# A hybrid block with a mixture of experts: another order of work on TensorE, fp32r slot tables, other PSUM banks for second blocks

## The chip, the cores and the metric

One core of a Trainium2 chip runs the whole program. The metric is the device time of one execution in microseconds (us), smaller is better. The kernel before takes 2412.09 us in the median of 3 runs (2403.3 to 2412.42).

A core has five engines with a queue of instructions each, which they work through in order: TensorE (PE, matrix products and transposes), VectorE (DVE), ScalarE (ACT), GpSimd (POOL) and SyncE (SP). An instruction that waits holds up everything behind it on its engine. SP issues most DMA transfers, POOL and ACT a few; a transfer waits until its buffer is free, and what stands behind it in that queue waits too.

## The reference

One layer over 2048 tokens of width 1024, with 256 context tokens, in float32. Cut to what matters:

```python
m  = silu(c) @ w_mod + b_mod            # six rows: sh1, sc1, g1, sh2, sc2, g2; the context has its own
hn = modulate(rmsnorm(h, g_norm1), sh1, sc1)
cn = modulate(rmsnorm(cx, g_norm1), csh1, csc1)
z  = hn @ w_in                          # u, v (512 each), q (256), r (512), k (256), v (512), gates (32)
# context: k, v, gates only; its two final states start the scans over the latent tokens
a_out = spatial_gating(z_u, z_v, ...)   # gelu, group norm, a 128x128 product per group and chunk
o     = gla_bidir(q, k, v, la_f, la_b, s_ctx_f, s_ctx_b)   # chunks of 64, states carried both ways
b_out = rmsnorm(o) * g_gla * silu(z_r)
h     = h + g1 * (concat([a_out, b_out]) @ w_out)
hn2   = modulate(rmsnorm(h, g_norm2), sh2, sc2)
# hierarchical MoE: best of 8 groups, the best 2 of its 8 experts, blocks of 128 tokens per expert
y = segment_sum(gate * (silu(x @ w1[e]) * (x @ w3[e])) @ w2[e])
out = rmsnorm(h + g2 * y, g_final)
```

## The kernel before

**Precision.** A float32 product is built from values split into a high and a low part of type fp32r: `mm3` (lines 84 to 86) issues high x high, high x low and low x high. ACT makes the high part (`split_w`, L80), DVE the low part by a subtraction (L81). Where rows are few, plain float32 products are used, for example for the ranks and slot tables of the routing.

**Tiles and stages.** The 2048 tokens are 16 tiles of 128 rows, numbered 0 to 15 (T is 15); the 2 tiles of the context are -2 and -1, and two tiles make a pair, -1 for the context and 0 to 7 for the rest. The order of the work is written out by hand, function by function, and each engine's queue follows it.

- *Prologue and stage A* (to about 505 us). `kv_mm` makes k, v and gate columns of one tile in 8 steps over the width, six products each; `zg_t` transposes the gate columns (`pz`), `lg_mm` makes the decay logits (`lg`, then ACT and DVE make `la`), `pb_mm` sums them (`pr_`, `pb`, `pd`), and `pkv_mm` makes the state update (`pkv`, then `sf` on DVE). `xtr(0, g)` transposes pair 0 into the operands `xh` and `xl`. `ua_split(i)` splits two raw tiles of the u and v weights (`raw`, four buffers, loaded at L443). Then a loop over pairs; the last `psx_mm`, `q_mm` and `r_mm` calls stand at L586 to L594.
- *Stage C* (505 to 766 us), tile 15 down to 0: `c_q`, `c_qt`, `c_att` (scores `paf`, `pab`, masked into `at`), `c_o` (`po`), `c_r`, `c_bt` (transposes `pbt`, copied to `mfc` and sent to memory as `mxD`). In between run the splits of the output weights, and the modulation vectors (`mod2`: a row `macc` is set to zero, gets a bias row by DMA at L725, and is summed up by two DVE instructions a step at L728).
- *Stage D* (to about 1031 us), again from tile 15 down: `d_load` fetches a tile of `mxD`, `d_split` makes its parts `mhd` and `mld`, `d_mm`/`d_mix` multiply by the output weights, `d_norm` normalises, `d_logit` and `d_route` choose experts, `d_rank` counts a token's place in its expert (`prk`, against a running count `coh`), and `d_tab` adds to the table `slots`, which holds for every slot of every expert the token and the gate: `at` (one-hot of the place) times `what` (one-hot of the expert, scaled by the token or by the gate). The last two tiles go side by side (`lanes`, L1139). The finished table gives `idx` and `gate`, and POOL gathers the first experts' rows with `idx` (L1163).
- *MoE*, 64 experts in turn. `xprep` transposes the gathered rows (128x128 each) into one pair of PSUM banks and splits them; `block` multiplies; `yevac` (L1218) empties the output banks `PY` with the gate. Seven experts have more than 128 tokens and so a second block: its `xprep` goes through `PY`, and its up-products accumulate in the banks `TP`, which the first blocks' `xprep` uses.

## Time and profile before

| | |
|---|---|
| median of 3 runs | 2412.09 us |
| profiled execution | 2410.06 us, span 2408.4 us |
| PE busy | 2259.7 us (94%) |
| DVE busy | 1932.1 us (80%) |
| ACT busy | 1437.3 us (60%) |
| POOL busy | 739.2 us (31%) |

The profile is of one execution. Its own time is 1.7 us above its span, and 2.0 us under the median of the runs. PE is busy for nearly all of the span, so what matters is where it is idle, and where its clock is granted at half: a busy PE at half clock takes twice as long for the same products.

### The profile page before, as it was taken

Reading aid. Unit: us, or ns where it says so; the run is one execution under the profiler, and the core shown is the slowest. Engines: PE = TensorE matmul, PEld = TensorE weight load, DVE = VectorE, ACT = ScalarE, POOL = GpSimd, SP = SyncE. Lnnn points to the kernel's source line nnn. Section 1 sums busy time; section 2 is a strip of 40 time slices with the busy share of each in tenths; the row PEclk is TensorE's granted clock in tenths of the full one; section 3 lists DMA queues with packets and bytes.
Section 4 is the critical chain, followed back from the end, with each engine's and each line's share of the span. In section 5 each row is a group of like instructions: output and inputs, shape, how many; then the busy total and the mean of one; then the engine's idle time right before and its main releaser. Section 6 shows DMA issues by size and latency. Waiting matters only on the chain.

```text
span 2408.4 us, 40084 instructions
## 1 busy us (share of the span) xinstructions
PE 2259.7 (94%) x11932; PEld 1860.0 (77%) x11932; DVE 1932.1 (80%) x4302; ACT 1437.3 (60%) x2731; POOL 739.2 (31%) x602
## 2 busy tenths in 40 slices
PE   8999999989999899899999999999999999999990
PEld 3888888977777788778777888888777788888870
DVE  4556665657786888789887899999686699999986
ACT  3544444432332222378676788888575688888873
POOL 1123311146673122237431222323131132322220
PEclk9899999989999999989999999999999999999995
DMA  7333322356675654589997899999996799999947
GB/s 274 105 107 106 121 92 97 109 170 210 219 241 175 227 210 159 184 323 374 323 310 259 292 377 372 365 352 348 325 327 194 223 360 373 368 358 363 360 140 296
DMA packets 193220, 613.42 MB, mean 255 GB/s; under 512 B 36557, under 2 KB 36685, under 8 KB 192854
## 3 DMA queue, kind: packets, MB, share of 16 engines
q1 hardware_dynamic: 152358, 516.56, 59.0%
q0 software_dynamic: 38048, 87.95, 12.4%
q10 hardware_dynamic: 2448, 4.46, 0.5%
q8 instruction: 178, 2.92, 0.5%
q14 instruction: 188, 1.54, 0.2%
HBM read 547.42 MB, written 102.28 MB: 270 GB/s over the span
## 4 chain that ended last, share of the span: by engine, by line
PE 35%; DVE 11%; DMA 6%; issue 5%; ACT 1%; DVEq 0%; another core or an unknown queue 0%; SPq 0%; POOLq 0%; ACTq 0%; POOL 0%
DVE wl L81 9%; PE pa L84 7%; PE pa L86 7%; PE pa L85 7%; DMA we<-in_w_e_dram 3%; PE py L84 2%; PE py L85 2%; PE py L86 2%; DMA accD<-y,idx 2%; PE tpe L1196 1%; PE tpe L85 1%; PE tpe L84 1%; PE tpe L86 1%; DVE y L1218 1%; ACT wh L80 1%
## 5 line engine op out<-in xcount | busy, mean ns | idle before, releaser
L81 DVE TENSOR_TENSOR wl<-we,wh 128x512 fp32r<-128x512 f32 x1536 | 967.6, 732 | 82.5 <-ACT wh L80 76.2
L80 ACT ACTIVATE wh<-we 128x512 fp32r<-128x512 f32 x1536 | 892.9, 630 | 146.3 <-DVE wl L81 46.3
L84 PE MATMUL pa<-wh,xhe 128*128 128x512 f32 x1024 | 404.2, 395 | 9.5 <-ACT wh L80 7.5
L1221 POOL DMA_INDIRECT accD<-y,idx x71 | 245.7, 3460 | 525.0 <-DVE y L1218 440.5
L86 PE MATMUL pa<-wh,xle 128*128 128x512 f32 x1024 | 400.4, 391 | 0.0
L85 PE MATMUL pa<-wl,xhe 128*128 128x512 f32 x1024 | 399.9, 391 | 0.0
L84 PEld LDWEIGHTS pa<-wh,xhe 128*128 128x128 f32 x1024 | 192.6, 188 | 69.9 <-issue 28.6
L86 PEld LDWEIGHTS pa<-wh,xle 128*128 128x128 f32 x1024 | 192.6, 188 | 41.0
L1163 POOL DMA_INDIRECT xg<-hnD,idx x64 | 96.5, 1508 | 410.7 <-DVE wl L81 124.9
L85 PEld LDWEIGHTS pa<-wl,xhe 128*128 128x128 f32 x1024 | 192.8, 188 | 37.6
L84 PE MATMUL py<-wh,hhe 128*128 128x512 f32 x512 | 213.5, 417 | 6.7 <-ACT wh L80 6.2
L86 PE MATMUL py<-wh,hle 128*128 128x512 f32 x512 | 202.7, 396 | 1.5 <-issue 1.3
L85 PE MATMUL py<-wl,hhe 128*128 128x512 f32 x512 | 201.1, 393 | 2.9 <-DVE wl L81 2.9
L86 PEld LDWEIGHTS py<-wh,hle 128*128 128x128 f32 x512 | 97.0, 190 | 25.3 <-issue 3.1
L351 POOL TENSOR_SCALAR sc<-sc,dec 64x128 f32<-64x128 f32 x140 | 111.1, 793 | 17.8 <-PE po L683 6.4
L84 PEld LDWEIGHTS py<-wh,hhe 128*128 128x128 f32 x512 | 97.4, 190 | 24.5 <-issue 6.1
L85 PEld LDWEIGHTS py<-wl,hhe 128*128 128x128 f32 x512 | 97.7, 191 | 16.0
L1071 POOL DMA_INDIRECT tabD<-pair,ri x32 | 70.0, 2189 | 91.4 <-DMA tabD<-pair,ri 59.0
L1218 DVE SCALAR_TENSOR_TENSOR y<-py,gate,g2b 128x512 f32<-128x512 f32 x128 | 93.0, 791 | 4.0 <-PE py L86 3.9
L86 PE MATMUL pmx<-hi,mld 128*128 128x512 f32 x224 | 89.0, 397 | 6.1 <-DVE mld L81 6.1
L84 PE MATMUL pmx<-hi,mhd 128*128 128x512 f32 x224 | 91.9, 410 | 1.7 <-ACT mhd L80 1.7
L85 PE MATMUL pmx<-lo,mhd 128*128 128x512 f32 x224 | 88.0, 393 | 0.0
(417 smaller groups left out, 4651.2 us busy)
## 6 DMA issues: line engine op xcount, KB each, us to landing
we<-in_w_e_dram SPq DMA_DIRECT2D x765, 512.0 KB, 9.9
wt<-in_w_modB_dram SPq DMA_DIRECT2D x32, 512.0 KB, 5.7
kve<-kveD SPq DMA_DIRECT2D x48, 256.0 KB, 5.5
wt<-in_w_modA_dram SPq DMA_DIRECT2D x16, 512.0 KB, 7.5
x<-in_x_dram SPq DMA_DIRECT2D x16, 512.0 KB, 3.8
xD<-xf POOLq DMA_DIRECT2D x32, 256.0 KB, 3.1
mfd<-mxD SPq DMA_DIRECT2D x16, 512.0 KB
xd<-in_x_dram SPq DMA_DIRECT2D x16, 512.0 KB, 5.0
```

The lines of the kernel that those rows point to most:

```text
L80: act.activation(hi, raw, AF.Copy)
L81: vec.tensor_tensor(lo, raw, hi.bitcast(F32), op=OP.subtract)
L84: pe.matmul(o, lh, wh, start=start, stop=False)
L85: pe.matmul(o, lh, wl, start=False, stop=False)
L86: pe.matmul(o, ll, wh, start=False, stop=stop)
L351: pool.tensor_scalar(s1[64:128, hs], s0[64:128, hs], dec[64:128, ci, h:h + 1], None, op0=OP.mult)
L1071: pool.indirect_dma_start(out=tabD, out_offset=bass.IndirectOffsetOnAxis(ap=ri[:, i:i + 1], axis=0), in_=pair[:, i], in_offset=None)
L1163: pool.indirect_dma_start(out=x, out_offset=None, in_=hnD, in_offset=bass.IndirectOffsetOnAxis(ap=ix, axis=0), bounds_check=S - 1, oob_is_ ...
L1196: pe.transpose(four(tp[c // 4])[:, c % 4], x[:, c * P:(c + 1) * P], ident)
L1218: vec.scalar_tensor_tensor(y[:, c], py[i], gt, g2b[:, c], op0=OP.mult, op1=OP.mult)
L1221: pool.indirect_dma_start(out=accD, out_offset=bass.IndirectOffsetOnAxis(ap=ix, axis=0), in_=y, in_offset=None, bounds_check=S - 1, oob_is ...
```

## The change

Six edits.

1. *Prologue.* `xtr(0, 0)`, `xtr(0, 1)`, `pkv_mm(t0)`, `kv_mm(0, 0)` and `pkv_mm(-1)` stand at other places among the context's steps.
2. *End of stage A.* `q_mm(14)` stands ahead of `psx_mm(7, 0)`, `psx_mm(7, 1)` stands in the middle of `r_mm(15)`; the first half of `r_mm(14)` is cut into two pieces, the second behind `c_att(15)`.
3. *End of stage C.* The products `d_mm(15, 0)` stand ahead of `c_o(0)` and `d_mm(15, 1)` ahead of `c_bt(0)`; the splits of tiles 15 and 14 are made a step earlier, and tile 13's `mfd` is loaded with them into a buffer of another pool.
4. *Slot tables.* `ot`, `coh`, `at`, `what` and two constant matrices become fp32r, so the products of `d_rank` and `d_tab` are fp32r. The gate is split into a high and a low column, so `what` has 192 columns where it had 128: more ACT instructions, one on DVE, and at the end one more to add the two parts.
5. *Last routing chain.* `warm` multiplies constants into banks that nothing reads: 5 products ahead of the last ranks, 1 ahead of the last tables, 3 behind the counts.
6. *Second blocks.* Their `xprep` goes through `TP` where it went through `PY`.

```diff
--- before.py
+++ after.py
@@ -469,23 +469,25 @@
     kv_mm(-1, 1, 0, 4)
     lg_mm(t0)
     ua_split(1)
-    xtr(0, 0)
     kv_mm(-1, 1, 4, KD)
     ptt = pt("aux", [P, 4, P], "ptt")
     for g in range(4):
         pe.matmul(ptt[:, g], lnb[:, g * P:(g + 1) * P], wsp[:, g], start=True, stop=False)
         pe.matmul(ptt[:, g], ones[0:1], bsp[:, g * P:(g + 1) * P], start=False, stop=True)
     vec.tensor_copy(tt, ptt)
-    xtr(0, 1)
+    xtr(0, 0)
     zg_t(t1)
     pb_mm(t0)
+    xtr(0, 1)
     ua_split(2)
     xtr(0, 2)
-    lg_mm(t1)
-    ua_split(3)
     pkv_mm(t0)
     xtr(0, 3)
     xload(1)
+    ua_split(3)
+    kv_mm(0, 0, 0, 4)
+    lg_mm(t1)
+    kv_mm(0, 0, 4, KD)
     pb_mm(t1)
     for i in range(4, 8):
         ua_split(i)
@@ -493,12 +495,12 @@
     for pr in range(NP):
         t0, t1 = 2 * pr, 2 * pr + 1
         nx = pr + 1 < NP
-        kv_mm(pr, 0, 0, KD)
         if pr:
+            kv_mm(pr, 0, 0, KD)
             psx_mm(pr - 1, 0)
-        else:
+        kv_mm(pr, 1, 0, 2)
+        if not pr:
             pkv_mm(-1)
-        kv_mm(pr, 1, 0, 2)
         zg_t(t0)
         kv_mm(pr, 1, 2, 4)
         if pr:
@@ -584,14 +586,15 @@
             mm3(RP[ti], *lhs(ti // 2, ti % 2, k), rh[k], rl[k], k == 0, k == KD - 1)
 
     q_mm(T)
+    q_mm(T - 1)
     psx_mm(NP - 1, 0)
-    q_mm(T - 1)
     c_kv(T)
     c_s0(T, 1)
     back(2 * (T + NCT) + 1, "kb")
     c_s0(T, 0)
+    r_mm(T, 0, 4)
     psx_mm(NP - 1, 1)
-    r_mm(T, 0, KD)
+    r_mm(T, 4, KD)
     es.close()
 
 
@@ -760,7 +763,12 @@
         oh_.append(hi)
         ol_.append(lo)
 
-    MX, MF, XR, PM = {}, [], {}, {}
+    MX, MF, MFD, XR, PM = {}, [], {}, {}, {}
+
+    def warm(o, n):
+
+        for _ in range(n):
+            pe.matmul(o, ident, cst[:, 0:512], start=True, stop=True)
 
     def d_x(ti, pl=None, tag="xd"):
         x = XR[ti] = (pl or wk).tile([P, D], F32, name="xd", tag=tag, **({} if pl else {"bufs": 2}))
@@ -780,12 +788,13 @@
     msk = cload("msk", [P, 2, P], dt=I32, p=wk)
     mod2_load(0)
     c_q(T)
-    r_mm(T - 1, 0, 4)
+    r_mm(T - 1, 0, 2)
     c_r(T)
     c_qt(T)
     c_kv(T - 1)
     c_st(T - 1)
     c_att(T)
+    r_mm(T - 1, 2, 4)
     for it in range(NT):
         ti = T - it
         n = ti - 1
@@ -795,6 +804,8 @@
             if it:
                 q_mm(n)
             c_q(n)
+        if n < 0:
+            d_mm(T, 0)
         c_o(ti)
         if n >= 0:
             if it:
@@ -812,7 +823,14 @@
             c_kv(n - 1)
             c_st(n - 1)
         if n < 0:
-            d_mm(T, 0)
+            d_mm(T, 1)
+        if it == NT - 2:
+            for i in range(2):
+                MX[T - i] = [wa.tile([P, KD, P], F32R, name=f"mx{j}", tag="w") for j in range(2)]
+                split_w(MF[i], *MX[T - i])
+                d_x(T - i, wa, "w")
+            MFD[T - 2] = wa.tile([P, KD, P], F32, name="mfd", tag="w")
+            sp.dma_start(out=MFD[T - 2], in_=mxD[T - 2])
         c_bt(ti)
         if n >= 0:
             c_att(n)
@@ -831,31 +849,27 @@
                 mf = wk.tile([P, KD, P], F32, name="mfd", tag="x", bufs=2)
                 sp.dma_start(out=mf, in_=mxD[T - i])
                 MF.append(mf)
-        if it == NT - 2:
-            for i in range(2):
-                MX[T - i] = [wa.tile([P, KD, P], F32R, name=f"mx{j}", tag="w") for j in range(2)]
-                split_w(MF[i], *MX[T - i])
-                d_x(T - i, wa, "w")
-    d_mm(T, 1)
     for j in range(2):
         d_mm(T - 1, j)
     es.close()
     p1s.close()
 
 
-    coh = const.tile([P, NE], F32, name="coh")
-    vec.memset(coh, 0.0)
+    coh = const.tile([P, NE], F32R, name="coh")
+    cohf = coh.bitcast(F32)
+    vec.tensor_scalar(coh, cst[:, 0:NE], 0.0, None, op0=OP.mult)
     zero = const.tile([P, 1], F32, name="zero")
     vec.memset(zero, 0.0)
     es = ExitStack()
     wk = es.enter_context(tc.tile_pool(name="p1d", bufs=1))
+    lor = wk.tile([P, 2, P], F32R, name="lor")
+    vec.tensor_copy(lor.rearrange("p t c -> p (t c)"), cst[:, 5 * P:7 * P])
+    lowr, onesr = lor[:, 0], lor[:, 1]
     bc = [wk.tile([P, D], F32, name=f"bc{i}") for i in range(2)]
     wr = wk.tile([P, KD, G + NE], F32, name="wr")
     br = wk.tile([P, G + NE], F32, name="br")
     iota = wk.tile([P, NE], F32, name="iota")
     HH, HN, HT = ({} for _ in range(3))
-
-    MFD = {}
 
     def d_load(ti):
         mf = MFD[ti] = wk.tile([P, KD, P], F32, name="mfd", tag="x", bufs=2)
@@ -1001,7 +1015,7 @@
         vec.tensor_tensor(oh, iota[:, None, :].to_broadcast([P, 2, NE]), ef[:, :, None].to_broadcast([P, 2, NE]),
                           op=OP.is_equal)
         yield
-        ot = wk.tile([P, NE], F32, name="ot", tag="ot", bufs=2)
+        ot = wk.tile([P, NE], F32R, name="ot", tag="ot", bufs=2)
         vec.tensor_tensor(ot, oh[:, 0], oh[:, 1], op=OP.add)
         yield
         RT[ti] = e2, se, ot, oh, ef
@@ -1010,13 +1024,13 @@
         e2, se, ot, oh, ef = RT[ti]
         dn = sm("dn")
         prk = pt("aux", [P, NE], "prk")
-        pe.matmul(prk, low, ot, start=True, stop=False)
+        pe.matmul(prk, lowr, ot, start=True, stop=False)
         for m in more_:
-            pe.matmul(prk, ones, m, start=False, stop=False)
-        pe.matmul(prk, ones, coh, start=False, stop=True)
+            pe.matmul(prk, onesr, m, start=False, stop=False)
+        pe.matmul(prk, onesr, coh, start=False, stop=True)
         pair = const.tile([P, 2, 2], F32, name="pair", tag="pair", bufs=3)
         pool.tensor_copy(pair[:, :, 0], tok[:, ti:ti + 1].to_broadcast([P, 2]))
-        what = wk.tile([P, 2, 2, NE], F32, name="what", tag="what", bufs=2)
+        what = wk.tile([P, 2, 3, NE], F32R, name="what", tag="what", bufs=2)
         act.activation(what[:, :, 0], oh, AF.Copy, scale=tok1[:, ti:ti + 1])
         vec.scalar_tensor_tensor(dn, e2, 1.0, se, op0=OP.add, op1=OP.mult)
         yield
@@ -1024,14 +1038,19 @@
         yield
         vec.tensor_tensor(pair[:, 1, 1:2], pair[:, 0, 1:2], e2, op=OP.mult)
         yield
+        gh, gl = wk.tile([P, 2], F32R, name="gh", tag="gh", bufs=2), sm("gl", 2)
+        act.activation(gh, pair[:, :, 1], AF.Copy)
+        vec.tensor_tensor(gl, pair[:, :, 1], gh.bitcast(F32), op=OP.subtract)
+        yield
         for i in range(2):
-            act.activation(what[:, i, 1], oh[:, i], AF.Copy, scale=pair[:, i, 1:2])
-        rk, at = sm("rk", 2), wk.tile([P, 2, 2 * P], F32, name="at", tag="at", bufs=2)
+            act.activation(what[:, i, 1], oh[:, i], AF.Copy, scale=gh[:, i:i + 1].bitcast(F32))
+            act.activation(what[:, i, 2], oh[:, i], AF.Copy, scale=gl[:, i:i + 1])
+        rk, at = sm("rk", 2), wk.tile([P, 2, 2 * P], F32R, name="at", tag="at", bufs=2)
         ri = const.tile([P, 2], I32, name="ri", tag="ri", bufs=3)
         prod = wk.tile([P, 2, NE], F32, name="prod", tag="prod", bufs=2)
         vec.tensor_tensor(prod, oh, prk[:, None, :].to_broadcast([P, 2, NE]), op=OP.mult)
         yield
-        vec.tensor_tensor(coh, coh, ot, op=OP.add)
+        vec.tensor_tensor(coh, cohf, ot.bitcast(F32), op=OP.add)
         yield
         vec.tensor_reduce(rk, prod, axis=AX.X, op=OP.add)
         yield
@@ -1078,7 +1097,7 @@
         if it > 1:
             d_x(ti)
         if it == 2:
-            slots = pt("mm", [P, 2, 2, NE], "slots")
+            slots = pt("mm", [P, 2, 3, NE], "slots")
             vec.memset(slots, 0.0)
         if it == 1:
             d_split(ti - 1)
@@ -1113,7 +1132,6 @@
             d_tr(ti + 1)
         ss = d_norm(ti, route)
         if it == 0:
-            d_load(T - 2)
             d_load(T - 3)
             pool.dma_start(out=hnD[0:P], in_=sh2b)
             sp.dma_start(out=sh2T, in_=bcD[1:2].rearrange("o (k p) -> p (o k)", p=P))
@@ -1136,8 +1154,11 @@
     rs0 = d_norm0(ss)
     for x in xgr + xqr:
         act.activation(x, zero.to_broadcast([P, D]), AF.Copy)
+    wm = pt("tp", [P, 512], "wm")
+    warm(wm, 5)
     lanes(g_route(1), g_route(0, rs0))
     lanes(g_rank(1), g_rank(0, RT[1][2]))
+    warm(wm, 1)
     d_tab(1)
     d_tab(0)
     wload(NW)
@@ -1147,7 +1168,9 @@
     none = wk.tile([P, 2, NE], F32, name="none")
     vec.tensor_scalar(none, slots[:, :, 0], 0.0, off, op0=OP.is_equal, op1=OP.mult)
     vec.scalar_tensor_tensor(idx.rearrange("p (b e) -> p b e", b=2), slots[:, :, 0], -1.0, none, op0=OP.add, op1=OP.add)
-    vec.tensor_copy(gate.rearrange("p (b e) -> p b e", b=2), slots[:, :, 1])
+    ghi = wk.tile([P, 2, NE], F32, name="ghi")
+    vec.tensor_copy(ghi, slots[:, :, 1])
+    vec.tensor_tensor(gate.rearrange("p (b e) -> p b e", b=2), ghi, slots[:, :, 2], op=OP.add)
     es.close()
 
 
@@ -1174,8 +1197,9 @@
     PA, TP, PY, TH = ([psp.tile([P, 512], F32, name=f"{n}{i}") for i in range(2)] for n in ("pa", "tpe", "py", "th"))
     four = lambda t: t.rearrange("p (c n) -> p c n", c=4)
     pc = TH[1][:, 0:NE]
-    pe.matmul(pc, ones, coh, start=True, stop=True)
+    pe.matmul(pc, ones, cohf, start=True, stop=True)
     ci_ = wk.tile([1, NE], I32, name="ci_")
+    warm(PA[1], 3)
     vec.tensor_scalar(ci_, pc[0:1], float(P - 1), None, op0=OP.add)
     vec.tensor_scalar(nblk, ci_, 7, None, op0=OP.logical_shift_right)
     most = wk.tile([1, 1], I32, name="most")
@@ -1317,7 +1341,7 @@
         base = hpos[e, 0, 0]
 
         def two():
-            xprep(xq[e % 2], rows2(e), PY)
+            xprep(xq[e % 2], rows2(e), TP)
             block(base, 2 * KD, (PA, TP), (xhl, rows2(e)), at)
             glu(PA, sh)
             glu(TP, sh2[e % 2])
```

**Where instructions stand, PE in the prologue.** Before, from the last of the bias products (`ptt`) to the first products of tile 0: `tp` are the transposes of `xtr`, `pz` of `zg_t`; `pr__` and `pd` belong to `pb_mm`.

```order
L477 MATMUL ptt<-bsp,cst 128x128
L213 MATMUL tp<-cst,x 128x128 x4
L254 MATMUL pz<-cst,kz 96x128
L278 MATMUL pr__599<-lah,trs 128x256
L278 MATMUL pr__599<-lal,trs 128x256
L278 MATMUL pr__599<-lah,trs 128x256
L278 MATMUL pr__599<-lal,trs 128x256
L287 MATMUL pd<-chm,la 128x2 x4
L213 MATMUL tp<-cst,x 128x128 x4
L259 MATMUL lg<-wup,zgT_178 128x512
L322 MATMUL pkv<-vv,kd 128x128 x8
L213 MATMUL tp<-cst,x 128x128 x4
```

After, from the same place:

```order
L476 MATMUL ptt<-bsp,cst 128x128
L213 MATMUL tp<-cst,x 128x128 x4
L254 MATMUL pz<-cst,kz 96x128
L278 MATMUL pr__586<-lah,trs 128x256
L278 MATMUL pr__586<-lal,trs 128x256
L278 MATMUL pr__586<-lah,trs 128x256
L278 MATMUL pr__586<-lal,trs 128x256
L287 MATMUL pd<-chm,la 128x2 x4
L213 MATMUL tp<-cst,x 128x128 x8
L322 MATMUL pkv<-vv,kd 128x128 x8
L213 MATMUL tp<-cst,x 128x128 x4
L84 MATMUL kg<-hi,xh 128x288
```

The first four transposes of pair 0 stood between the two halves of `kv_mm(-1, 1)` before, and now all sixteen stand behind it; `lg` has moved behind the first half of `kv_mm(0, 0)`, which begins at the last row.

**SP at the start of stage D.** Before, from the last loads of stage C: `mfd` are tiles of `mxD`, `wt` weights of the modulation, `macc` the bias row.

```order
L832 DMA mfd<-mxD 128x1024 x2
L767 DMA xd<-in_x_dram 128x1024 x2
L872 DMA bc_8286<-bcD 128x1024
L872 DMA bc_8287<-bcD 128x1024
L880 DMA wr<-in_w_r_dram 128x576
L883 DMA iota<-in_iota_dram 128x64
L884 DMA br<-in_b_r_dram 128x72
L713 DMA wt_8311<-in_w_modB_dram 128x1024
L713 DMA wt_8313<-in_w_modB_dram 128x1024
L862 DMA mfd<-mxD 128x1024 x2
L1119 DMA sh2T<-bcD 128x8x1
L725 DMA macc<-in_b_mod_dram 1x1024
```

After:

```order
L775 DMA xd<-in_x_dram 128x1024 x2
L833 DMA mfd<-mxD 128x1024
L886 DMA bc_8290<-bcD 128x1024
L886 DMA bc_8291<-bcD 128x1024
L894 DMA wr<-in_w_r_dram 128x576
L897 DMA iota<-in_iota_dram 128x64
L898 DMA br<-in_b_r_dram 128x72
L716 DMA wt_8315<-in_w_modB_dram 128x1024
L716 DMA wt_8317<-in_w_modB_dram 128x1024
L876 DMA mfd<-mxD 128x1024
L1137 DMA sh2T<-bcD 128x8x1
L728 DMA macc<-in_b_mod_dram 1x1024
```

One of the two `mfd` loads ahead of `sh2T` has moved up, ahead of the `bc` loads; the rest keep their order.

**PE at the end of the routing.** Before, from the last logits (`pl`) to the first expert's transposes (`tpe`):

```order
L945 MATMUL pl<-wr,ht 128x72 x8
L1013 MATMUL prk<-ot,cst 128x64
L1016 MATMUL prk<-coh,cst 128x64
L1013 MATMUL prk<-ot,cst 128x64
L1015 MATMUL prk<-ot,cst 128x64
L1016 MATMUL prk<-coh,cst 128x64
L1064 MATMUL slots<-what,at 128x128 x8
L1177 MATMUL th_11189<-coh,cst 128x64
L1279 TENSOR_LOAD nblk x2
L1196 MATMUL tpe_11184<-cst,xg_10935 128x128 x4
```

After:

```order
L959 MATMUL pl<-wr,ht 128x72 x8
L771 MATMUL wm<-cst 128x512 x5
L1027 MATMUL prk<-ot,lor 128x64
L1030 MATMUL prk<-coh,lor 128x64
L1027 MATMUL prk<-ot,lor 128x64
L1029 MATMUL prk<-ot,lor 128x64
L1030 MATMUL prk<-coh,lor 128x64
L771 MATMUL wm<-cst 128x512
L1083 MATMUL slots<-what,at 128x192 x8
L1200 MATMUL th_11296<-coh,cst 128x64
L771 MATMUL pa_11290<-cst 128x512 x3
```

Three groups of constant products are new, and the tables' products have 192 columns.

## Rows read from the trace of the kernel before

**Rows 1.** Timeline of PE in the prologue: start, duration, what, idle time and releaser.

```profile
58.99 1.47 PE L213 MATMUL tp<-cst,x 128*128 128x128 f32 x4 [2.61 <-DVE x L195]
...
77.61 2.07 PE L322 MATMUL pkv<-vv,kd 64*128 64x128 f32 x14 [3.18 <-DVE la L265]
```

**Rows 2.** Busy time by stretch: stretch, length, engines, granted clock, DMA share, GB/s.

```profile
58.24:65.07 6.83, 5.96 (x20) 5.11 (x21) 4.88 (x8) 2.67 (x6) 0.80 (x1) 0.50 0.26 82
75.30:88.95 13.65, 10.75 (x46) 9.57 (x47) 9.71 (x22) 8.68 (x17) 2.24 (x4) 0.50 0.56 179
```

**Rows 3.** Timeline of DVE in the prologue: the last weight splits.

```profile
91.46 1.36 DVE L81 TENSOR_TENSOR lo<-raw,hi 128x512 fp32r<-128x512 f32 x2 [0.24 <-ACT hi L80]
```

**Rows 4.** Timeline of PE where stage A ends.

```profile
506.56 2.05 PE L395 MATMUL psx<-wsp,ga 128*128 128x128 f32 x8 [3.73 <-DVE sf L335]
...
522.23 0.60 PE L659 MATMUL pqt<-cst,qe 128*128 128x128 f32 x4
```

**Rows 5.** Timeline of DVE at the same place.

```profile
511.95 1.12 DVE L401 SCALAR_TENSOR_TENSOR mf<-psx,lng,tt 128x128 f32<-128x128 f32 x4
...
519.00 0.76 DVE L649 SCALAR_TENSOR_TENSOR qe<-pq,kve 128x256 f32<-128x256 f32 x2 [3.16 <-POOL sc L352]
```

**Rows 6.** Timeline of PE at the end of stage C.

```profile
755.61 0.46 PE L681 MATMUL po<-kve,at 128*128 128x128 f32 x2 [2.19 <-issue]
```

**Rows 7.** Timeline of SP at the start of stage D.

```profile
766.20 0.81 SPq L872 DMA_DIRECT2D bc<-bcD  x2
...
778.38 0.25 SPq L725 DMA_DIRECT2D macc<-in_b_mod_dram  x1
```

**Rows 8.** Timeline of DVE at the start of stage D.

```profile
786.90 2.60 DVE L728 SCALAR_TENSOR_TENSOR macc<-wt,sig,macc 128x1024 f32<-128x1024 f32 x2 [8.55 <-DMA macc<-in_b_mod_dram]
789.42 1.22 DVE L81 TENSOR_TENSOR mld<-mfd,mhd 128x1024 fp32r<-128x1024 f32 x1
```

**Rows 9.** Busy time by stretch: the start of stage D, its steady part.

```profile
774.00:787.00 13.00, 8.90 (x43) 6.93 (x41) 4.11 (x8) 2.03 (x3) 1.06 (x2) 0.93 1.03 403
791.00:1011.00 220.00, 218.08 (x1215) 188.24 (x1215) 181.21 (x704) 63.80 (x156) 54.56 (x71) 0.99 0.51 187
```

**Rows 10.** Timeline of PE in stage D: one table, and what follows it.

```profile
974.09 1.06 PE L1064 MATMUL slots<-what,at 128*128 128x128 f32 x8
974.98 0.38 PE L934 MATMUL tpd<-cst,hn 128*128 128x128 f32 x2
```

**Rows 11.** Timeline of PE in stage D: one tile's ranks, and what follows.

```profile
981.37 0.33 PE L1013 MATMUL prk<-ot,cst 128*128 128x64 f32 x2
...
981.75 0.51 PE L945 MATMUL pl<-wr,ht 128*128 128x72 f32 x3
```

**Rows 12.** Timeline of PE: fp32r products of 256 columns in a row.

```profile
500.06 0.28 PE L86 MATMUL pq<-hi,xl 128*128 128x256 f32 x1
500.18 0.28 PE L84 MATMUL pq<-hi,xh 128*128 128x256 f32 x1
```

**Rows 13.** Timeline of PE in the last routing chain.

```profile
1018.57 0.69 PE L1013 MATMUL prk<-ot,cst 128*128 128x64 f32 x2 [4.75 <-DVE ot L1005]
...
1022.48 3.75 PE L1064 MATMUL slots<-what,at 128*128 128x128 f32 x16 [1.51 <-DVE at L1039]
...
1031.48 1.97 PE L1196 MATMUL tpe<-cst,xg 128*128 128x128 f32 x8 [3.53 <-DMA xg<-hnD,idx]
```

**Rows 14.** Busy time by stretch: from the last ranks into the first expert.

```profile
1017.38:1037.86 20.48, 13.19 (x47) 11.25 (x48) 12.84 (x47) 9.09 (x25) 6.25 (x8) 0.50 0.53 154
```

**Rows 15.** Waits of PE, 1050 to 2336 us: total, times, longest.

```profile
PE py L1196 <- issue: 7.5, 5, 1.5
...
PE py L1196 <- DVE y L1218: 2.2, 2, 1.3
```

**Rows 16.** Timeline of DVE at one second block.

```profile
1249.04 1.41 DVE L1218 SCALAR_TENSOR_TENSOR y<-py,gate,g2b 128x512 f32<-128x512 f32 x2
```

**Rows 17.** Busy time by stretch: experts with one block.

```profile
1050.00:1170.00 120.00, 119.08 (x556) 97.42 (x556) 119.93 (x200) 104.66 (x188) 83.19 (x19) 1.00 1.01 375
```

## The prediction

> **What bounds the kernel now.** I read the view of busy time by stretch first, because PE is busy for 94% of the span and an average over stages hides where it is not. In the steady part of stage D it works for 218.08 of 220 us at a granted clock of 0.99 [rows 9], and among experts with one block for 119.08 of 120 us, where DVE is busy for 119.93 us and the DMA share is 1.01 [rows 17]. In both, time comes off the end only where PE's own work shrinks. [...] A gain ahead of the experts is worth its size at the end, if weights and splits can move up with it; a rival says what if not.
>
> **The change part by part.** The sum is made against the profiled execution, 2410.06 us (span 2408.4), which is 2.0 us under the median of the runs.
>
> *Prologue.* PE idles 2.61 us before the transposes of pair 0 and 3.18 us before `pkv`, at half clock around both [rows 1, 2]. The order after does the same work up to the gates of tile 0, but puts the context's second half of `kv_mm` into the first hole and products of `kv_mm(0, 0)` where `lg` stood alone. If nothing else is late, this gives 2.61 + 3.18 = 5.8 us of idle time, plus half the busy time at half clock, (5.96 + 10.75) / 2 = 8.4 us: 14.2 us at most. What is late next is DVE: the gates of tile 0 now come up for PE earlier, but their copy stands on DVE behind the last weight splits and the state update. The splits end at 91.46 + 1.36 = 92.8 us, waiting for raw weights [rows 3]. The eight loads reuse buffers that earlier splits free, and these come some 4 us earlier in my walk through the order, so the splits end at about 89, and with eight updates behind them PE waits some 3 us and runs at half clock for a while after. If the splits don't move, 4 us are left of the gain. I take **8 us**, bounds 4 and 14.
>
> Of the clock: the row shows half clock for 13.65 us from 75.30 on, after a run of transposes and very narrow products and an idle time of 3.18 us [rows 1, 2]. [...]
>
> *End of stage A.* PE idles 3.73 us before `psx` [rows 4]. `q_mm(14)`, 24 products of 500.18 - 500.06 = 0.12 us [rows 12], 2.9 us, now lies in that hole. But `qe` waits for DVE's `mf`, which starts at 511.95, and for a chain through POOL that lets it start at 519.00 [rows 5]; no edit moves that chain. So the transposes of `qe` can come from 522.23 to about 519.8 at best, 2.4 us. The second piece of `r_mm(14)`, 6 products of twice that width, some 1.4 us, then covers part of the wait for the masked scores. I take **4 us**, bounds 2 (only the first) and 6 (the full clock kept as well).
>
> *End of stage C.* `d_mm(15, 0)` fills the 2.19 us before `po` [rows 6]. What it costs: `c_bt(0)` now stands behind 24 products of `d_mm(15, 1)`, 24 x 0.23 = 5.5 us (0.23 is an estimate: twice the 0.12 of 256 columns), so the last `mfc` on ACT, for which stage D's first loads wait on SP (766.20), comes about 5.5 - 1.4 = 4 us later. Behind these loads stands the bias row `macc` (778.38), for which DVE idles 8.55 us; both sums on `macc` and then `mld` of tile 13 follow, ending at 789.42 + 1.22 = 790.6 us, where PE resumes [rows 7, 8]. The DMA engines are full here (share 1.03, 403 GB/s) [rows 9]; the early `mfd` takes 0.5 MB out of that queue, 0.52 / 403 GB/s = 1.3 us. So PE resumes at 790.6 + 4 - 1.3 = 793.3: a **loss of 2.5 us**, bounds a gain of 2.2 (the chain moves up by as much as the filled hole) and a loss of 6 (moves back by all of `d_mm(15, 1)`).
>
> *Slot tables.* A table takes PE 974.98 - 974.09 = 0.89 us, four float32 products of 128 columns, 0.22 us each [rows 10]; a tile's ranks 981.75 - 981.37 = 0.38 us [rows 11]. No row shows an fp32r product under 256 columns. Nearest is the one of 256, 0.12 us [rows 12]: at that price a table of 192 columns takes at most 4 x 0.12 = 0.48 us, and ranks at most 2 x 0.12 = 0.24. That saves 0.41 + 0.14 = 0.55 us a tile, for 14 tiles ahead of the last chain 7.7 us. Where PE isn't the end for a moment it is lost; I take **7 us**. If a narrow fp32r product goes at the float32 rate, a table takes 0.89 x 192 / 128 = 1.34 us, and 14 of them lose 6.3 us; if cost falls with columns all the way, ranks 0.06 and tables 0.36, 14 x 0.85 = 12 us are saved. Bounds: -6 to 12. [...] The added ACT and DVE instructions lie in ACT's 156 and DVE's 39 idle us of these 220 [rows 9]; without that cover each would cost its length.
>
> *Last routing chain.* PE idles 4.75 us before the ranks, 1.51 before the tables, 3.53 before the first expert's rows [rows 13], and is granted half clock for 20.48 us with 13.19 us busy [rows 14]. Five constant products, each 4 x 0.22 = 0.89 us (512 columns at the float32 rate), fill 4.4 us of the first hole and end before the ranks' input is there, so the chain on DVE and ACT keeps its times. It shortens where PE is in it: the tables, 3.75 us at half clock [rows 13], take about 1 at full clock as fp32r, and ranks 1 less; two more ACT columns per tile take some back. So the gathers start about 3.5 us earlier, and of the 6.4 us until 1037.86 that the first expert runs at half clock [rows 13, 14], half is saved, 3.2. Together 6.7; I take **6 us**, bounds 2 (clock lost anyway) and 8.
>
> *Second blocks.* Seven times PE waits with a second block's transposes for `PY`, which DVE must empty first: 7.5 + 2.2 = 9.7 us in seven waits [rows 15]; at the block shown DVE needs until 1249.04 + 1.41 = 1250.45 [rows 16]. `TP` has been emptied by then. New: the first products into `TP` must wait until ACT and DVE have emptied it of these transposes, with DVE busy until 1250.45 and two subtractions of 0.6 us behind that, 1251.7; PE, some 1.2 us earlier, is there at 1252.2 by my count. Just enough. I take **8.5 us**, bounds 0 and 9.7.
>
> Sum: 8 + 4 - 2.5 + 7 + 6 + 8.5 = 31.0 us, and 2410.06 - 31.0 = **2379 us**.
>
> **The rivals.**
> 1. *Everything closes*: the prologue gives 14, tables 12, stage C's edge nothing lost: 14 + 4 + 0 + 12 + 7 + 9 = 46, 2364 us. For it speaks that these are the rows' own upper ends; against it, that DVE's splits [rows 3] stand in the way.
> 2. *Given back at the seams*: the clock stays at half in the prologue (gain 4, no more), narrow products save nothing, stage D starts 6 us late: 4 + 3 - 6 + 0 + 5 + 8.5 = 14.5, 2396 us. For it speak the macc chain and the DMA share there [rows 8, 9].
> 3. *The experts' weights set the end*: if the stream of weights, at a DMA share of 1.01 [rows 17], cannot move up, only part of the gain in front and of the second blocks' counts, some 6 us: 2404 us. Against it, PE waits for neither weights nor splits in those experts [rows 15, 17].
> 4. *Slower*: `TP` as the bottleneck. If a weight split stands on DVE ahead of the two subtractions, or ACT is late with its halves, PE stands in the second block until `TP` is empty. Seven blocks must lose all that the rest gains: (31 - 8.5) / 7 = 3.2 us each for no change, and with 8 us each the time is 2410 - 22.5 + 56 = 2444. From 5 us a block on it is over 0.5% slower. Against it: in the order, the subtractions stand right behind DVE's `y`.
>
> **How the numbers follow.** A measurement of this kernel can tell about 0.5%, 12 us, from no change. Chances: forecast 0.55 (2370 to 2388), rival 1 0.12, rival 2 0.20, rival 3 0.09, rival 4 0.04. Forecast and rival 1 are faster, and most of rival 2 (0.17); rival 3 and the rest of rival 2 are within 0.5%: 0.12; rival 4 gives slower 0.03 and 0.01 to no change. So faster 0.84, same 0.13, slower 0.03. The range takes in rivals 1 and 2 and ends before 3: 2363 to 2401 us.
>
> **What would show it.** Right: the granted clock near 1 from 1014 us on and no wait of 4 us before `prk`; the table under 0.5 us; no wait on the second blocks' transposes and none before their first products into `TP`; PE resuming at about the same distance from the start of `pmx` or later than before in stage D. Wrong: a table over 0.89 us; half clock in all of the prologue; DVE waiting for `macc` as long as before with PE 10 us idle or more there; an expert with one block longer than before.

## The result and the profile after

The changed kernel takes 2387.09 us in the median of 10 runs (2379.48 to 2399.08) against 2410.0 us before (10 runs, 2399.61 to 2412.42): a ratio of 0.9914, 95% interval 0.9897 to 0.9931, so 20.7 us faster (17 to 25); the two medians lie 22.9 us apart. Forecast were 31 us. The profiled execution, 2381.12 us, is one of the fast ones of its kind; against the profiled 2410.06 us of before it is 28.9 us faster. Both numbers matter below: the seams of the profile, the stretches in which PE waits or is granted half clock, add up nearly as forecast, and the median of the runs shows 8 to 10 us less than the forecast.

PE's row of busy time on the page:

```profile
PE 2240.5 (94%) x11853; PEld 1839.4 (77%) x11853; DVE 1932.1 (81%) x4320; ACT 1447.2 (61%) x2779; POOL 744.7 (31%) x602
```

Busy time by stretch in the prologue, at the start of stage D and ahead of the first expert (stretch, length, busy time of PE, PEld, DVE, ACT, POOL, then granted clock, DMA share, GB/s):

```profile
57.45:64.27 6.82, 6.82 (x39) 5.45 (x39) 4.89 (x11) 3.47 (x9) 0.00 (x0) 1.00 0.23 71
64.27:71.10 6.83, 6.41 (x36) 5.70 (x36) 3.46 (x9) 4.15 (x9) 1.40 (x2) 0.50 0.19 69
94.99:98.41 3.42, 3.42 (x12) 2.85 (x12) 1.15 (x2) 2.57 (x7) 0.00 (x0) 0.50 0.00 0
774.24:787.89 13.65, 4.94 (x12) 3.87 (x13) 6.95 (x18) 3.50 (x5) 0.53 (x1) 0.50 0.96 373
1009.78:1013.19 3.41, 3.41 (x6) 1.86 (x7) 0.69 (x4) 0.70 (x2) 2.56 (x3) 0.50 0.20 48
```

Of the 20.5 us at half clock in the prologue [rows 2] 10.2 are left, and of those from the last ranks into the first expert [rows 14] 3.4 of 20.5. The timeline of PE (start, duration, what, idle time and releaser) at the seams, from the prologue to the first expert:

```profile
94.11 0.47 PE L259 MATMUL lg<-wup,zgT 98*128 98x512 f32 x1 [3.86 <-DVE zgT L255]
...
505.00 1.16 PE L395 MATMUL psx<-wsp,ga 128*128 128x128 f32 x8 [0.73 <-DVE ga L388]
513.88 0.63 PE L662 MATMUL pqt<-cst,qe 128*128 128x128 f32 x4 [3.52 <-DVE qe L652]
...
782.95 0.79 PE L86 MATMUL pmx<-hi,mld 128*128 128x512 f32 x1 [11.96 <-DVE mld L81]
...
961.00 0.58 PE L1083 MATMUL slots<-what,at 128*128 128x192 f32 x4
961.42 1.04 PE L948 MATMUL tpd<-cst,hn 128*128 128x128 f32 x8
967.80 0.19 PE L1027 MATMUL prk<-ot,lor 128*128 128x64 f32 x1
967.82 0.27 PE L1030 MATMUL prk<-coh,lor 128*128 128x64 f32 x1
967.93 1.98 PE L959 MATMUL pl<-wr,ht 128*128 128x72 f32 x16
...
999.23 4.50 PE L771 MATMUL wm<-cst 128*128 128x512 f32 x10
1004.17 0.30 PE L1027 MATMUL prk<-ot,lor 128*128 128x64 f32 x1 [0.43 <-DVE ot L1019]
1006.99 1.41 PE L1083 MATMUL slots<-what,at 128*128 128x192 f32 x8 [1.13 <-DVE at L1058]
1014.33 1.04 PE L1220 MATMUL tpe<-cst,xg 128*128 128x128 f32 x8
```

Against [rows 1, 4, 6, 10, 11, 13]: the waits before `tp`, `pkv`, `psx`, `po`, `prk` and `tpe` are gone or short, a table takes 0.42 us where it took 0.89, a tile's ranks 0.13 where they took 0.38. New are 3.86 us before `lg`, 3.52 before `pqt`, and 11.96 us where stage D starts. DVE and SP there answer to [rows 7, 8]; the first two rows are DVE, the last is SP:

```profile
779.16 2.61 DVE L731 SCALAR_TENSOR_TENSOR macc<-wt,sig,macc 128x1024 f32<-128x1024 f32 x2 [9.34 <-DMA macc<-in_b_mod_dram]
781.68 1.22 DVE L81 TENSOR_TENSOR mld<-mfd,mhd 128x1024 fp32r<-128x1024 f32 x1
```

```profile
769.84 0.26 SPq L728 DMA_DIRECT2D macc<-in_b_mod_dram  x1
```

In the experts, PE's waits (total, times, longest) answer to [rows 15]. The waits of the second blocks' transposes fell from 9.7 us in seven to 3.7 in two; `th`, the first transposes of a second block ahead of its down products, now has three waits that PE's own issue ended, where before it had one. The first two rows are of the changed kernel, the third of the one before:

```profile
PE th L1228 <- issue: 7.8, 3, 4.5
...
PE tpe L1220 <- DVE y L1242: 3.7, 2, 2.1
```

```profile
PE th L1204 <- issue: 4.3, 1, 4.3
```

What "issue" is there, PE's sequencer tells in part. Its conditional branches (count, then min/median/max in ns) in the changed kernel, ahead of an expert's down products (L1379) and ahead of its up products (L1354), then in the kernel before, ahead of the down products:

```profile
L1379 PEldq COMPARE_BRANCH  x121: 64/176/5221, 1038.6 to 2320.5; - x121
```

```profile
L1354 PEldq COMPARE_BRANCH  x121: 64/176/3842, 1014.2 to 2301.4; - x121
```

```profile
L1355 PEldq COMPARE_BRANCH  x121: 64/176/1490, 1058.3 to 2349.2; - x121
```

A branch that takes 0.18 us in the median takes 5.22 us at 1197.8, into the second block of the 9th expert (down products), 3.84 and 2.80 us at the 12th (up, then down products) and 2.31 us at the 14th (down). Before, none is above 1.5 us among the experts; but the 4.34 us that PE waits before `th` there, until 1905.3, stand right behind a branch of 0.21 us into the second block of the 40th. So the length of the branches is not the whole of it.

What these stops have in common is in the view of the DMA queues, among them q8, whose kind is "instruction". It brings packets of 16 KB (0.02 MB in the row; over the whole span of the changed kernel 2.90 MB in 177 packets). In the changed kernel one runs from 1200.6 to 1201.6 us, while PE stands at the branch of 5.22 us (first row, 1200 to 1201), and in the kernel before one from 1902.1 to 1904.1 us, while PE waits before `th` (second row, 1902 to 1903):

```profile
q8 instruction: 1, 0.02, 6.6%
```

```profile
q8 instruction: 1, 0.02, 12.7%
```

PE goes on 1.4 and 1.2 us after they have landed. Ahead of the first expert's transposes q8 brings 47 packets in either kernel, where PE has 11,984 and 12,142 instructions, so 255 and 258 to a packet, waits and branches not counted. From these numbers I take q8 for PE's stream of instructions, and such a stop for PE waiting for its next ones; no view names the instructions in a packet. This was in no step of the prediction.

### The profile page after: what moved, and what is told of

It is laid out like the page before. It is cut to its first block, busy times and chain, and to the rows that moved or that the text cites. A ratio compares the mean times of both kernels' runs of the same rounds, so it can differ in the third digit from the quotient of the medians.

```text
span 2379.4 us, 39981 instructions
## 1 busy us (share of the span) xinstructions
PE 2240.5 (94%) x11853; PEld 1839.4 (77%) x11853; DVE 1932.1 (81%) x4320; ACT 1447.2 (61%) x2779; POOL 744.7 (31%) x602
## 5 line engine op out<-in xcount | busy, mean ns | idle before, releaser
L81 DVE TENSOR_TENSOR wl<-we,wh 128x512 fp32r<-128x512 f32 x1536 | 954.8, 686 | 74.4 <-ACT wh L80 71.9
L1090 POOL DMA_INDIRECT tabD<-pair,ri x32 | 75.6, 2363 | 96.0 <-DMA tabD<-pair,ri 58.2
```

The lines of the kernel that those rows point to most:

```text
L81: vec.tensor_tensor(lo, raw, hi.bitcast(F32), op=OP.subtract)
L1090: pool.indirect_dma_start(out=tabD, out_offset=bass.IndirectOffsetOnAxis(ap=ri[:, i:i + 1], axis=0), in_=pair[:, i], in_offset=None)
```

## The experiments

The theory after the result: each edit is worth what its seam shows, and the rest of the forecast was lost to PE's branches in the experts. The medians of before that stand beside these runs are 2408.8 to 2410.0 us. All edits are on the changed kernel unless said.

**Once more, unchanged.**

> The changed kernel itself, once more. Two theories on why its ten runs spread from 2379 to 2399 us, where the profiled one (2381) shows four branches of PE's sequencer in the experts of 2.3 to 5.2 us (1197.8, 1233.8, 1277.9 and 1333.6 us), ahead of a second block's code. Theory A: how long such a branch takes is decided anew in each execution, and with it the clock behind it. Then the profile shows long branches at other places or of other lengths, and the time again lies anywhere between 2379 and 2399. Theory B: the layout of the program decides it. Then the same four places are late by the same 2.3 to 5.2 us. Everything ahead of the experts should agree with the profile at hand within 1 us: pair 0's first psx at 138.7, PE resuming in stage D at 783, the first expert's transposes at 1014.3 us.

Measured: 2389.15 us (6 runs, 2377.62 to 2391.27). The branches are long at the same experts: 5.30 us at the 9th, 6.20 and 2.36 at the 12th (the 14th's was not). Theory B, layout, for the places; the sizes vary. Ahead of the experts the profile agrees within 2.5 us, not 1: the prologue alone was 2.1 us shorter.

**Second blocks through PY.**

```diff
-            xprep(xq[e % 2], rows2(e), TP)
+            xprep(xq[e % 2], rows2(e), PY)
```

> The changed kernel, but the second blocks' transposes go through PY again, as before. My theory: the seven waits for PY come back, 0.8 to 1.6 us each and 9.6 us in all, less 2 us for the one wait that TP did not take away, so the experts (from the first tpe to the last pa) take 7 to 9 us longer, leaving aside branches of more than 1 us; all ahead of 1014 us stays. Rival: the switch of banks gained nothing by itself, since other waits in the experts (the branches) take its place; then the experts take the same time within 3 us.

Measured: 2405.23 us (12 runs), 16 slower than with TP, and the experts take 1312.3 us in the profile for 1288.2, 24 more. Both theories missed: the waits for PY are back, 9.8 us in seven, but the long branches (5.0, 5.35 and 5.2 us at the 9th, 12th and 14th expert) cost more as well, and half clock in the experts lasts 23.9 us where it lasted 6.8.

**Tables in float32.** (`ot`, `coh`, `at`, `what` in F32, 128 columns, the two constant matrices from `cst`.)

```diff
-        what = wk.tile([P, 2, 3, NE], F32R, name="what", tag="what", bufs=2)
+        what = wk.tile([P, 2, 2, NE], F32, name="what", tag="what", bufs=2)
```

> The changed kernel, but ranks and slot tables in plain float32 with 128 columns as before; the constant products stay. My theory: a table takes 0.89 us of PE again where it takes 0.33 or so as fp32r, ranks 0.38 for 0.22, so stage D from PE's resumption to the last logits is 6 to 8 us longer (216.2 us in the changed kernel's profile), and the last chain another 1 to 2. In all 7 to 9 us slower. Rival: DVE and ACT set the period of a tile, and PE only waits where it worked; then stage D is the same within 2 us.

Measured: 2388.43 us (6 runs), no slower than the repeat's 2389.15. Yet the stage did what I expected: from PE's resumption to the last logits it took 223.4 us for 216.2. The transposes `tpd` of two tiles follow at 15.01 us here, at 14.31 us with fp32r:

```profile
949.54 1.04 PE L946 MATMUL tpd<-cst,hn 128*128 128x128 f32 x8
964.55 1.04 PE L946 MATMUL tpd<-cst,hn 128*128 128x128 f32 x8
```

No branch of this kernel was longer than 1.2 us before the last expert, and this I took for what gave it back. The profile doesn't bear that out: the experts take 1286.8 us for 1288.1, since PE waits 4.78 us before `th` at the 14th expert and 2.47 us in the down products of the 12th, both behind branches of 0.22 us. The profiled execution (2383.0 us) is slower than those of the changed kernel (2381.1 and 2377.6); what made the medians equal is in no trace. In the trace a float32 product stands twice (128 `slots` records before, 64 in the changed kernel), so this PE queue is 194 instructions longer ahead of the experts (5986 products and as many weight loads, for 5889). The stops had moved with it, which pointed to the layout.

**No constant products.**

```diff
-    warm(wm, 5)
...
-    warm(wm, 1)
...
-    warm(PA[1], 3)
```

> The changed kernel without the nine constant products in the last routing chain. My theory: they keep the clock up. Without them PE idles 4.5 to 5 us before the last ranks, the granted clock falls to half for 10 to 20 us, ranks and tables take 2 us longer, and the first expert starts 1 to 3 us later and runs some 6 us of products at half clock: 4 to 6 us slower. Rival: the chain on DVE and ACT sets the time and the clock comes back at once; then within 1 us up to the first expert's transposes, and 2 us slower at most.

Measured: 2393.82 us (6 runs), 4.7 slower than the repeat, though the intervals overlap (ratios to before of 0.9915 to 0.9962, and 0.9897 to 0.9945). Half clock from 1003.0 to 1023.5 us, the wait before `prk` is 4.77 us again, but from the last logits to the first expert's transposes it takes 15.8 us for 15.2: with the products half clock lasts 3.4 us there, and the chain hardly moves. So my theory holds for the clock, with less in the chain than I gave. The 4.7 us can't be put down to it: the queue is also 36 instructions shorter, PE waits 4.10, 3.94 and 4.73 us before `th` at the 9th, 12th and 14th expert, and the experts take 1298.0 us for 1288.1.

**Padding of PE's queue.**

```diff
+    zb = wk.tile([P, 2], BF, name="zb")
+    vec.memset(zb, 0.0)
...
+    pd0 = pt("tp", [P, 2], "pad0")
+    for _ in range(88):
+        pe.matmul(pd0[0:2], zb, zb, start=True, stop=True)
```

> The changed kernel with 88 tiny extra products (2 columns, of zeros, into a bank that nothing reads) at the very start of PE's queue, where PE waits for its first weights until 5.6 us: 176 more instructions stand ahead of everything else on PE. Between the kernel before and the changed one PE's queue is shorter by some 158 instructions ahead of the experts. Theory B (layout): the long branches of PE into the second blocks' code (5 us at the experts around 1195, 1232 and 1278 us in two profiles of the changed kernel, none there in that of before, nor with the float32 tables, which have 194 instructions more) go away or move to other experts; with none of them left the experts take 5 to 10 us less (1288 now) and the median falls by about as much, to 2380. Theory A (each execution anew): the long branches are there as often, experts 1288 and the median 2388, both within 4. What lies ahead of the experts stays within 2 us.

Measured: **2373.49 us** (4 runs, 2371.7 to 2375.37), ratio to before 0.9863 (0.9841 to 0.9886). Theory B, with more than I gave: 2380 was expected. The experts take 1278.5 us, 9.6 less, no branch into a second block is above 1.2 us, and PE's waits there lost the row of `th` and that of the second blocks' `tpe`. The branch row, and the experts as a stretch, changed kernel and padded:

```profile
L1384 PEldq COMPARE_BRANCH  x121: 64/176/1651, 1039.2 to 2311.3; - x121
```

```profile
1014.33:2302.45 1288.12, 1265.36 (x5912) 1033.46 (x5911) 1187.52 (x1942) 1023.52 (x1805) 388.53 (x148) 1.00 0.93 331
```

```profile
1015.00:2293.50 1278.50, 1264.36 (x5913) 1033.29 (x5911) 1186.99 (x1942) 1024.10 (x1805) 388.81 (x148) 1.00 0.94 333
```

**The kernel before, padded the other way** (the same edit on it, with 49 products).

> The kernel before with 49 of the tiny products at the start of PE's queue, 98 instructions. With the 158 by which its queue is longer than the changed kernel's ahead of the experts this makes 256. If the place of PE's code within pages of 256 instructions decides how long the branches to the second blocks take, this kernel has the changed kernel's places: branches of 2 to 6 us at the 10th, 12th or 13th expert, where its profile without the padding has none over 1.5 us, and the median goes up by 6 to 14 us, to 2415 to 2424. Rival: the padding itself (PE at work before its first weights) was what helped the changed kernel; then this one gets faster, by 5 to 15 us. If neither, within 4 us of 2410.

Measured: 2420.34 us (6 runs), ratio to before 1.0046 (1.0028 to 1.0064): 11 us slower. Branches of 5.62, 4.63 and 5.12 us at the 9th, 12th and 14th expert (counted from one; the expectation's 10th and 13th are the 9th and the 12th), and `th` waits again. So padding itself helps nothing (the first `psx` comes 0.1 us later than without it); where the code lies does.

```profile
L1360 PEldq COMPARE_BRANCH  x121: 64/176/5621, 1055.9 to 2357.5; - x121
...
PE th L1209 <- issue: 13.2, 3, 4.9
```

**PY, padded** (the edits of the second and the fifth experiment).

> The changed kernel with the 88 tiny products at the start of PE's queue, and with the second blocks' transposes through PY as before. Against the padded kernel with TP (2373.5 us) the worth of the banks alone, with PE's branches short in both. My theory: seven waits for PY of 1.3 us, 9.7 us in all, and the clock mostly kept: experts 1278.5 + 9 = 1286 to 1290 us, median 2381 to 2386. Rival: the switch saves the 16 us by which the medians without padding differ (2405 against 2389); then the median is about 2389.

Measured: 2394.11 us (5 runs), 20.6 slower than padded with TP; I had expected 8 to 12, the rival 16. The seven waits for PY are 7.5 + 2.2 = 9.7 us, exactly those of before; but branches of 5.37 and 4.81 us now stand at the 34th and the 40th expert, with `th` waits of 4.60 and 4.24 us, and half clock for 10.2 us behind them. Waits are instructions too, EVENT_SEMAPHORE in the traces: from the first `tpe` to the last `pa` PE has 253 of them with PY (the profile before) and 265 with TP (the changed kernel's). That a padding which suits one does not suit the other for this reason is argued, not shown.

**Split of tile 13 ahead of the sums on macc.**

```diff
         if it == 1:
             d_split(ti - 1)
+            mod2(NQ)
...
-        if it < 4:
+        if 1 <= it < 4:
             mod2(NQ + it)
```

> The changed kernel with one step moved: the first two sums on macc in stage D stand on DVE behind the split of tile 13 (mld), where they stood ahead of it. My theory: PE's idle time of 12.0 us in stage D is DVE standing in front of mld for macc's bias row, which lands late in a full DMA queue; mld's inputs are there earlier. Then PE resumes 6 to 11 us earlier (783 us now), the clock may stay at full there (13.7 us at half now), and the median falls by 5 to 10 us. Rival: tile 13's mfd or its high part on ACT is what comes late; then PE resumes within 3 us of now.

Measured: 2386.05 us (6 runs), 3 less than the repeat, within its noise. PE resumes at 771.1 for 783.0, 12 us earlier, and the last logits come at 1001.7 for 999.1. The wait moved: `macc`'s row is still late, and what stands behind it on DVE now is the next tile's `hd` (first three rows DVE, the last PE):

```profile
769.41 1.22 DVE L81 TENSOR_TENSOR mld<-mfd,mhd 128x1024 fp32r<-128x1024 f32 x1
...
779.48 2.60 DVE L731 SCALAR_TENSOR_TENSOR macc<-wt,sig,macc 128x1024 f32<-128x1024 f32 x2 [7.78 <-DMA macc<-in_b_mod_dram]
782.00 1.28 DVE L915 TENSOR_TENSOR hd<-pmx,xd 128x512 f32<-128x512 f32 x2
```

```profile
782.74 0.80 PE L84 MATMUL pmx<-hi,mhd 128*128 128x512 f32 x1 [4.65 <-DVE hd L915]
```

**Late splits in the prologue.**

```diff
     pb_mm(t1)
-    for i in range(4, 8):
-        ua_split(i)
...
         lg_mm(t0)
+        if not pr:
+            for i in range(4, 8):
+                ua_split(i)
         kv_mm(pr, 1, 6, KD)
```

> The changed kernel with the last four weight splits of the prologue (ua_split 4 to 7) moved behind the gates of tile 0, so the state update and zgT don't stand behind them on DVE. My theory: PE's idle time of 3.9 us before lg (94 us) goes, and the half clock of 3.4 us behind it: the first u product comes 3 to 5 us earlier (97.9 now) and the median falls by as much. Rival: the splits are then late for the u and v products or for tile 1's gates, and PE waits there instead: first psx within 2 us of 138.6.

Measured: 2390.32 us (6 runs), the repeat's within noise. The rival: the first u product comes 6.0 us earlier, but the first `psx` 6.7 us later. Tile 1's gates now stand behind the splits on DVE:

```profile
103.37 0.42 PE L254 MATMUL pz<-cst,kz 128*96 128x128 f32 x1 [8.51 <-DVE kz L245]
```

**Padding, tile 13 first and late splits together.**

> The last three edits together on the changed kernel: padding of PE's queue, mld ahead of macc, late splits. If each is worth what I expect and they add up (they lie in different stages): 2388 less 7 (branches), 7 (mld) and 4 (splits) = 2370, between 2362 and 2378. If long branches are decided anew in each execution and only the two others count: 2377 us.

Measured: 2377.44 us (4 runs, 2372.02 to 2381.29): the padding counts, the other two do not. The number lies in the range that I gave, but by luck: the three together are 4 us above the padding alone, where I had expected 11 below it, and the long branches, with which the second theory came to 2377, are not there (none into a second block above 2.1 us).

**macc's row ahead of stage D's first loads, padded.**

```diff
-        if k0 == 0:
+        if k0 == 0 and grp < 3:
...
+    macc = wa.tile([P, D], F32, name="macc", tag="w")
+    vec.memset(macc, 0.0)
+    sp.dma_start(out=macc[0:1], in_=a["b_mod"][:, 5 * D:6 * D])
     coh = const.tile([P, NE], F32R, name="coh")
```

> The padded changed kernel, with macc's bias row loaded (and its buffer cleared) ahead of stage D's first loads, where it stood behind them; the sums on macc stay ahead of mld on DVE. My theory: DVE's idle time ahead of the sums is the row's late landing in a full DMA queue; moved up, it lands before 770 us and PE resumes when mld is there, 5 to 10 us earlier than 780.6, without the later waits that moving mld alone ran into (there the three first tile periods together stayed at 61 us). Median 2373.5 less 4 to 10. Rival: the weights wt that the sums also read land as late as the row; then PE resumes within 3 us of 780.6.

Measured: 2369.26 us (5 runs), 4.2 less than the padding alone, though the intervals touch (ratios to before of 0.9816 to 0.9843, and 0.9841 to 0.9886); PE resumes at 775.8 for 780.6. My theory at its lower end: the row no longer waits, but the weights `wt` do, for 2.87 and 0.96 us.

**macc's row early and tile 13 first, padded.**

> The padded changed kernel with both: macc's row ahead of stage D's first loads, and the sums behind mld. If the row alone was late, as above, but mld also first: PE resumes at 770 to 774 (780.6 with the padding alone), the first three tile periods fall from 61 to 50 to 55 us, and the median is 2362 to 2368. If the weights wt are what is late, the wait moves to the next tile's hd again and the median stays within 3 us of 2373.5.

Measured: **2364.82 us** (5 runs, 2362.49 to 2368.13), ratio to before 0.9819 (0.9805 to 0.9832), the fastest version: 44.6 us under before, 8.7 under the padding alone. PE resumes at 770.7, and the first three tile periods take 53.8 us for 61.6, both as expected. On DVE, the sums wait 1.5 us where they waited 9.3:

```profile
769.07 1.22 DVE L81 TENSOR_TENSOR mld<-mfd,mhd 128x1024 fp32r<-128x1024 f32 x1
770.47 1.28 DVE L736 SCALAR_TENSOR_TENSOR macc<-wt,sig,macc 128x1024 f32<-128x1024 f32 x1 [0.18 <-DMA wt<-in_w_modB_dram]
773.02 1.28 DVE L736 SCALAR_TENSOR_TENSOR macc<-wt,sig,macc 128x1024 f32<-128x1024 f32 x1 [1.27 <-DMA wt<-in_w_modB_dram]
```

## Why the prediction was right, and what it lacked

Step by step, from the two profiles (start of the same instruction, before and after):

- *Prologue*, forecast 8: the first `psx` comes 7.3 us earlier (145.9, 138.6). What I named as late next is what is late: DVE's `zgT` behind the weight splits, 3.86 us, with 3.4 us of half clock behind it. The parts came otherwise than I had them: the splits end at 91.7 us, 1.1 earlier and not 4, and of the 5.8 us of idle time 1.7 are gained; the rest is half clock, 10.2 us shorter, which is worth some 5, an estimate (eight transposes `tpe` took 1.97 us at half clock [rows 13], 1.04 at full). Half clock did come in the prologue, as rival 2 had it, from 64.27 to 71.10 us, through the transposes, `pr_`, `pd` and `pkv`.
- *End of stage A*, forecast 4: about 3.5. The last `pkv` is 5.1 us earlier (2 us are lost on the way; a half clock of 3.4 us at 248.6 that the profile before does not have is not the cause, since the repeat has none there and loses 1.7), the first `pbt` 8.6. The chain to `qe` did hold `pqt` back, 3.52 us.
- *End of stage C*, forecast a loss of 2.5: the last `pqt` is 10.4 us earlier, PE's resumption 7.75 (790.70, 782.95), a loss of 2.6 us, by the chain I named. One of the signs that I gave for being wrong did come: DVE waits 9.34 us for `macc`, where it waited 8.55, and PE is idle for 11.96. It is part of the loss that the sum already had. The three experiments on `macc` show that its row, in a full DMA queue (a share of 1.05 and 403 GB/s from its issue at 769.84 to 779.16 us), was the cause, and the weights behind it the next one.
- *Slot tables*, forecast 7: 6.7 us from the resumption to the last logits (222.8, 216.2). A narrow fp32r product costs less than I allowed: 0.10 us for 192 columns, 0.06 for 64. At these prices a tile saves 0.72 us and 14 tiles 10 us, where I had 0.55 and 7.7. The steady tiles got it (15.02 to 14.31 us from one `tpd` to the next), the first one after the resumption nothing, and the third lost 1.2 us. So 7 was near by two misses that cancel.
- *Last chain*, forecast 6: 2.7 us to the first transposes (17.9, 15.2), and by the half clock that the first expert no longer has (6.4 us before) about 3 more, an estimate: half of it.
- *Second blocks*, forecast 8.5: the waits are worth 9.7 us, as the padded pair shows, which has them with PY and not with TP. In the profile two of the seven waits seem to have stayed, 3.7 us. One of these (1237.94) is behind a branch of 3.84 us at the 12th expert, the other ends 1.2 us after a packet of q8, and both are gone in the padded kernel: I take them for stops for instructions, so that all seven waits for the bank went.

These are 8.5 to 10 us for the second blocks, with 7.3, 3.5, -2.6, 6.7 and 5.7 for the rest: 29 to 31, and the profile has 28.9. What the sum lacked is a term that no edit names: PE's stops for instructions in the experts. Taken apart there, PE's idle time (waits of over 0.3 us, in the profiles, with the half clock beside it) is:

| us in the experts | all | waits for PY | stops that end behind a packet of q8 | half clock |
|---|---|---|---|---|
| before | 1300.1 | 9.6 | 9.9 | 13.2 |
| changed | 1288.1 | 0 | 11.9 | 6.8 |
| changed, tables in float32 | 1286.8 | 0 | 9.5 | 10.2 |
| changed, padded | 1278.5 | 0 | 3.8 | 3.4 |
| changed, PY | 1312.3 | 9.8 | 17.6 | 23.9 |
| changed, PY, padded | 1301.6 | 9.7 | 11.4 | 10.2 |
| before, padded | 1311.3 | 9.8 | 17.1 | 22.4 |

So the kernel before had such stops too, and the changed one loses only 2 us more by them in its profile. From the forecast of 2379 us to the median of 2387.1 there are 8 us: 2 to the profiled execution (2381.1), and 6 from there to the median. What the slower executions lose (up to 2399 us, at a mean granted clock of 0.970 to 0.977 for 0.978 in the profiled one), and where, no trace shows. Where the code lies can do as much: the padding takes 14 to 16 us off the median of the changed kernel (2387 to 2389, 2373.5), 9.6 of it in the profile's experts, and a padding of another length puts 11 on the kernel before. But the 35 us from before to the padded kernel (2409 - 2373.5) are not the edits alone, since 6 us of stops that the kernel before had are gone with them. So the range and the sign were right, and the terms nearly; two of them, prologue and tables, by parts that were off against each other. Rival 2, with 14.5 us of gain, came near the result for the wrong reasons: the seams gave nothing back beyond the forecast.

That a place in the code decides where PE stops is shown. The four kernels with 11,984 instructions of PE ahead of the experts and `TP` all stop ahead of both products of the 9th and of the 12th expert, for 1.5 to 4.5 us each; the four with 176 more stop for over 2 us only in the 14th, for 2.3 to 2.6. The kernel before with its 98 has 12,240, just 256 more than the changed one with PY, and these two stop at the same three experts, for 5.62, 4.63 and 5.12 us at the branch in one and 5.0, 5.35 and 5.2 in the other. On why, the traces have this much: each stop of over 1 us ends 1.2 to 1.8 us after a packet of 16 KB on q8 has landed, and 256 instructions more, about what a packet brings here (255 and 258 by the counts above), give the same places. That PE waits at these stops for its next instructions is argued from this, not shown. Why a place is a good one, and why a stop can stand behind a branch as well as in it, stays open.

## What to carry to other kernels

Where a program branches, a change ahead of the branch moves the code behind it (here by 158 of PE's instructions): compare the waits that an engine's own issue ended, its longest branches and the packets of its instructions in both profiles before a gain or a loss is put down to an edit, and try a padding of the queue at a place where the engine is idle anyway (here PE's first 5.6 us, where a padding took the median from 2389.15 to 2373.49 us, and one of another length added 11 us to the kernel before). When a stall's cause is a late transfer, moving one victim from behind it can move the wait to the next instruction on that engine, as here from `mld` (11.96 us of PE's time) to `hd` (4.65 us, and a median only 3 us lower, within the noise); move the transfer first, then the order, which here gave 4.2 and 4.4 us. An experiment that changes the number of instructions measures its edit and the layout together (PY for TP cost 16 us without padding and 20.6 with it), and only a profile by stage tells them apart.

## What the runs showed of the hardware

- In the experts of the fourteen profiles PE waits 73 times for more than 1 us. Of these, 24 are a second block's first transposes waiting for `PY`. Each of the other 49, whether the view of the waits has it as issue, DVE or ACT, ends 1.2 to 1.8 us after a packet of q8 has landed; of the 24, two do. One of the 49 is the 4.85 us before `py` at 2336.83 us in the kernel before, which the view puts down to ACT's `wh`, 1.7 us after a packet. So I take a wait of this kind that seems to be for DVE or ACT for one for instructions.
- The clock fell to half at 64.27 us with PE busy for all of the 6.82 us ahead of it: 3.1 us of `kv` products, 3.1 of `ptt`, whose float32 products have 128 columns, and 0.6 of transposes. Which of these, if any, was the cause, this stretch doesn't tell.
- Ten runs of one kernel spread over 20 us, and their mean granted clock with them: 0.978 in a run of 2381 us, 0.970 in one of 2399. The padded kernel's four runs lie within 3.7 us.
